# Moving the steps of the pattern weights apart by a group of units, and loading query and key rows twice

## The chip, the cores and the metric

One core of a Trainium2 chip runs one layer of an encoder trunk. The metric is the device time of one execution in microseconds. TensorE (PE) multiplies matrices and transposes, VectorE (DVE) and ScalarE (ACT) work on tiles, GpSimd (POOL) too, and SyncE (SP) issues nearly all transfers (DMAs). Each engine takes its instructions in order; an instruction that has to wait holds up those behind it.

## The reference

For 2048 tokens of width 1024 (float32): RMSNorm and one input projection, whose columns go half to attention and half to a gated recurrence (HGRN2). Both results together go through an output projection, and a mixture of 16 experts follows. The change lies in the attention:

```python
for window, dilation in ((128, 1), (512, 4), (2048, 16)):
    m, den, num = dilated_window_attention(qh, kh, vh, window, dilation, slopes)
    ms.append(m); dens.append(den); nums.append(num)
m_all = jnp.stack(ms)
scale = jnp.exp(m_all - jnp.max(m_all, axis=0, keepdims=True))
numer = jnp.sum(scale[..., None] * jnp.stack(nums), axis=0)
denom = jnp.sum(scale * jnp.stack(dens), axis=0)
return (numer / denom[..., None]).reshape(B, S, ATTN_WIDTH)
```

There are 8 heads of width 64. For each head and token the three patterns give a maximum, a denominator and a numerator. The weight of a pattern is `scale` divided by `denom`.

## The kernel before

Products in float32 are made of three products of high and low halves. The low halves of the activations (`hlo`) lie in DRAM (`lo_d`) and are loaded through a ring of 9 buffers, four for each block of 256 tokens.

The program text does not fix the order on the engines. It is handed to a planner (`schedule_with_timeline_sim=True`, L1307), which issues what is ready in its own reckoning by priority. Priorities come from lanes, in which the text counts them upwards: `first`, `feed` (loads and preparation of projections), `mixer` (recurrence and attention), `fill` (matmuls of projections, which use PE where the mixer leaves it idle).

Attention goes head by head (`att_head`). Within a head, g = 0 to 3 are groups of 512 tokens. `four(pat, n4, ...)` handles four units of 128 queries: scores on PE, table and minimum on DVE (L661), exponential on ACT (L662), transposes on PE (L664), copies (L666, L668), products with the values (L694), and the numerator out of PSUM (L697 to L701). A group has a `four` of pattern 0 and one of pattern 1; all four of pattern 2 come at the end of g = 1. That makes 12 to a head.

The weights of a group of tokens take this way: the statistics of patterns 0 and 2 are stored to DRAM (`st_d`, L758 and L782), because they come out in another arrangement of tokens than is wanted. `weights(g)` loads them (`sg`, L711), works out the weights on DVE and ACT (L717 to L723, tile `cw` with two buffers), stores these (`cw_d`, L724) and loads them spread over the partitions (`wB`, two buffers, L727, two loads). `combine(g)` multiplies and adds on POOL (L732 to L735) and stores the result to `mixt_d` (L737), which the output projection reads later.

`after(k)`, k = 0 to 7, stands after each `four` of patterns 0 and 1. The dictionary `late` says what comes there: `weights(0)` and `weights(1)` at 4, `combine(0)` at 5, `combine(1)` and `weights(2)` at 6; `weights(3)`, `combine(2)` and `combine(3)` at 0, 1 and 2 of the next head.

Query and key rows of the next head come by `att_load` (L538): 128 partitions x 4 rows of 64 floats into the left half of a tile `x4` (four buffers). `att_twice` (L546) copies them on POOL into the right half. `att_turn` transposes the tile on PE (L576), and ACT and DVE write the queries (`qs`, L580, L581) and the high and low halves of the keys (`kh`, `kl`, L585, L586). `queries` copies queries on POOL (`qc`, L620, L623). While heads run, PE fills with projections (L236 to L238) and with the first half of the output projection (`op_mm`, L859 to L861).

Of the kernel before, what the change touches and what calls it, by code (L numbers as in the profile page):

```python
# [23 lines left out]
F32 = mybir.dt.float32  # L24
F32R = mybir.dt.float32r
# [20 lines left out]
def encoder_layer(ctx, tc, x, norm1_w, w_in, q_norm_w, k_norm_w, lb_f, lb_b, o_norm_w, w_out,  # L46
# [80 lines left out]
    def phase0(g):  # L127

        xs = []
        for i in range(2):  # L130
            t = g * 2 + i
            xt = xp.tile([128, D], F32, name="xt", bufs=8)
            sp.dma_start(xt, x[0, t * 128:(t + 1) * 128, :])
            xs.append(xt)
        for xt in xs:
            ss = xp.tile([128, 1], F32, name="ss", bufs=4)
            y = xp.tile([128, 1], F32, name="ssy", bufs=4)
            tm = xp.tile([128, 1], F32, name="sst", bufs=4)
            junk = xp.tile([128, D], F32, name="junk", bufs=2)
            act.activation(junk, xt, AF.Square, accum_out=ss)  # L140
            dve.tensor_scalar(ss, ss, 1.0 / D, EPS, op0=OP.mult, op1=OP.add)
            rsqrt(y, ss, tm)
            dve.tensor_scalar(xt, xt, y, None, op0=OP.mult)
        sl = slice(g * 256, (g + 1) * 256)
        lot = []
        for k in range(0, KC, 2):
            p = (pa, pb)[k // 2 % 2]()
            for j in range(2):
                for i in range(2):
                    c = (2 * j + i) * 128  # L150
                    pe.transpose(p[:, c:c + 128], xs[i][:, (k + j) * 128:(k + j + 1) * 128], ident)
            pv = p.rearrange("p (k t) -> p k t", k=2)
            act.activation(hth[:, k:k + 2, sl], pv, AF.Copy)  # L153
            lo = ring.tile([128, 2, 256], F32R, name="hlo", bufs=9)
            dve.tensor_sub(lo, pv, hth[:, k:k + 2, sl].bitcast(F32))
            sp.dma_start(lo_d.rearrange("k p s -> p k s")[:, k:k + 2, sl], lo.bitcast(F32))
            lot.append(lo)
        return lot
# [44 lines left out]
    def project(cols, kind, ev, begin=False):  # L203

        lots = []
        with (first if begin else feed)():
            if begin:
                lots.append(phase0(0))
            pieces = [prep(cols, kc) for kc in range(KC)]
        for g in range(8):  # L210
            lot = []
            if begin:
                if g < 7:
                    with first():
                        lots.append(phase0(g + 1))
                lot = lots[g]
            with feed():
                for k2 in range(len(lot), 4):
                    t = ring.tile([128, 2, 256], F32R, name="hlo", bufs=9)
                    sp.dma_start(t.bitcast(F32), lo_d.rearrange("k p s -> p k s")[:, k2 * 2:k2 * 2 + 2, g * 256:(g + 1) * 256])  # L220
                    lot.append(t)

            p = pm()
            for b in range(2):
                bs = slice(b * 128, (b + 1) * 128)
                with fill():
                    o = p[:, b * 256:(b + 1) * 256]
                    for kc in range(KC):
                        hi, lo = pieces[kc]
                        hs = hth[:, kc, g * 256:(g + 1) * 256]  # L230
                        ls = lot[kc // 2][:, kc % 2, :]
                        if kind == "t":
                            l, r = (hs[:, bs], ls[:, bs]), (hi, lo)
                        else:
                            l, r = (hi[:, bs], lo[:, bs]), (hs, ls)
                        pe.matmul(o, l[0], r[0], start=kc == 0, stop=False)  # L236
                        pe.matmul(o, l[0], r[1], start=False, stop=False)  # L237
                        pe.matmul(o, l[1], r[0], start=False, stop=kc == KC - 1)  # L238
            with feed():
                ev(g, p)  # L240
# [259 lines left out]
    def att_setup(p):  # L500
# [13 lines left out]
            pool.dma_start(wq[s * 64:(s + 1) * 64, :], q_norm_w.rearrange("o d -> d o"))  # L514
            pool.dma_start(wk[s * 64:(s + 1) * 64, :], k_norm_w.rearrange("o d -> d o"))
        dve.tensor_scalar(wq, wq, -0.125, None, op0=OP.mult)
        T["wq"], T["wk"], T["late"] = wq, wk, {}
        T["qs"] = p.tile([128, S], F32R, name="qs", bufs=1)

        for n in ("kh", "kl"):  # L520
# [11 lines left out]
    def att_load(p, T, h, g):  # L532

        u, s2 = h // 2, h % 2
        for j in range(2):

            x4 = p.tile([128, 4, 128], F32, name="x4", bufs=4)
            sp.dma_start(x4[:, :, :64],  # L538
                         dram_ap(qk_d, (u * S + g * 512) * 256 + 128 * j + 64 * s2,
                                 [[256, 128], [128 * 256, 4], [1, 64]]))  # L540
            T["x4", g, j] = x4

    def att_twice(T, g):
        for j in range(2):
            x4 = T["x4", g, j]
            pool.tensor_copy(x4[:, :, 64:], x4[:, :, :64])  # L546

    def att_values(T, h, g):

# [41 lines left out]
    def att_head(p, T, h):  # L591
# [113 lines left out]
        qcs = {(0, 0): queries(0, 0), (1, 0): queries(1, 0)}  # L705
        late = T["late"]

        def weights(g):
            sg, wB, nt = grp[g]
            for a in (0, 1):  # L710
                sp.dma_start(sg[:, 2 * a].rearrange("p t c -> p (t c)"),  # L711
                             dram_ap(st_d, ((a * 8 + h) * S + 512 * g) * 2, [[8, 128], [1, 8]]))
            w = p.tile([128, 3, 4], F32, name="cw", bufs=2)
            m8 = p.tile([128, 4], F32, name="cm", bufs=2)
            d8 = p.tile([128, 4], F32, name="cd", bufs=2)
            wd = p.tile([128, 3, 4], F32, name="cdd", bufs=2)
            dve.tensor_reduce(m8, sg[:, :, :, 1].rearrange("p a t -> p t a"), axis=AX.X, op=OP.min)  # L717
            dve.tensor_tensor(w, m8[:, None, :].to_broadcast([128, 3, 4]), sg[:, :, :, 1], op=OP.subtract)
            act.activation(w, w, AF.Exp)
            dve.tensor_mul(wd, w, sg[:, :, :, 0])  # L720
            dve.tensor_reduce(d8, wd.rearrange("p a t -> p t a"), axis=AX.X, op=OP.add)
            dve.reciprocal(d8, d8)
            dve.tensor_mul(w, w, d8[:, None, :].to_broadcast([128, 3, 4]))  # L723
            sp.dma_start(dram_ap(cw_d, h * 3 * S + 512 * g, [[4, 128], [S, 3], [1, 4]]), w)  # L724
            wB = p.tile([128, 3, 256], F32, name="wB", bufs=2)
            for hf in range(2):
                sp.dma_start(wB[64 * hf:64 * hf + 64], dram_ap(cw_d, h * 3 * S + 512 * g + 256 * hf, [[0, 64], [S, 3], [1, 256]]))  # L727
            grp[g] = sg, wB, nt

        def combine(g):  # L730
            sg, wB, nt = grp.pop(g)
# [7 lines left out]

        grp = {}  # L740

        def after(k):

            for f in late.pop(k, []):
                f()

        for g in range(4):
            sg = p.tile([128, 3, 4, 2], F32, name="sg", bufs=4)
            nt = p.tile([128, 2, 256], F32, name="nt", bufs=3)
            grp[g] = sg, None, nt  # L750
            st0 = p.tile([128, 4, 2], F32, name="st0", bufs=2)
            if g == 0:
                att_twice(T, 2)
                att_twice(T, 3)
            elif g > 1 and h < 7:
                att_twice(T, g - 2)
            four(0, 4 * g, st0, nt[:, 0])
            sp.dma_start(dram_ap(st_d, (h * S + 512 * g) * 2, [[2, 128], [256, 4], [1, 2]]), st0)  # L758
            after(2 * g)
# [17 lines left out]
            if g == 1:  # L777
# [4 lines left out]
                sp.dma_start(dram_ap(st_d, (8 + h) * S * 2, [[32, 128], [1, 32]]), st2.rearrange("p r c -> p (r c)"))  # L782
                if h < 7:
                    att_v2(T, h + 1)
                late[4] = [lambda: weights(0), lambda: weights(1)]
                late[5] = [lambda: combine(0)]
                late[6] = [lambda: combine(1), lambda: weights(2)]
            if g and h < 7:
                att_values(T, h + 1, g - 1)
                if g == 3:  # L790
                    att_values(T, h + 1, 3)
        late[0] = [lambda: weights(3)]
        late[1] = [lambda: combine(2)]
        late[2] = [lambda: combine(3)]
        if h == 7:
            for k in range(3):
                after(k)


    def op_setup(op):  # L800
        T = {"op": op}
        T["wh"] = op.tile([128, KC, D], F32R, name="woh", bufs=1)
        T["wl"] = op.tile([128, KC, D], F32R, name="wol", bufs=1)

# [17 lines left out]
    def op_weights(T, half):  # L822
        for k in range(4 * half, 4 * half + 4):
# [2 lines left out]
            act.activation(T["wh"][:, k, :], raw, AF.Copy)  # L826
            dve.tensor_sub(T["wl"][:, k, :], raw, T["wh"][:, k, :].bitcast(F32))

    def op_mm(T, c, half, src):

        op = T["op"]
        r = slice(c * 128, (c + 1) * 128)
        with feed():
            mt = op.tile([128, 512], F32, name="mx", bufs=2)
            mtv = mt.rearrange("p (k t) -> p k t", k=4)
            if half:
                sp.dma_start(mt, mix_d[r, :])
            else:
                sp.dma_start(mtv, mixt_d[c // 4].rearrange("(k p) s -> p k s", p=128)[:, :, c % 4 * 128:c % 4 * 128 + 128])
            xt = op.tile([128, D], F32, name="oxt", bufs=3)  # L840
            sp.dma_start(xt, src[r, :])
# [112 lines left out]
    with mixer():  # L954
# [3 lines left out]
        for g in range(4):  # L958
            att_load(ap_, AT, 0, g)
            att_values(AT, 0, g)  # L960
            if g < 2:
                att_twice(AT, g)
                att_turn(AT, g)
    heads(0)
    unit_qk(2)
# [5 lines left out]
    octx = ExitStack()  # L971
    op = octx.enter_context(tc.tile_pool(name="op", bufs=1, side="right"))
    with feed():
        OT = op_setup(op)
        op_weights(OT, 1)
    for c in range(NT):
        op_mm(OT, c, 1, x[0])
# [333 lines left out]
```

## Time and profile before

| | us |
|---|---|
| median of 3 runs | 2851.4 |
| lowest, highest | 2849.88, 2853.11 |
| the profiled execution | 2847.59 |
| its span, first to last instruction | 2845.8 |

| engine | busy us | share of the span |
|---|---|---|
| PE | 2648.8 | 93% |
| DVE | 1779.0 | 63% |
| ACT | 1461.0 | 51% |
| POOL | 329.7 | 12% |

The shares are means over stages with different limits. The projections and the recurrence run to about 860 us, attention with projections beside it from there to about 1480, the output projection and the choice of tokens to about 1700, the experts from there to the end. A wait is read from the instruction that waits and the one that released it.

### The profile page before, as it was taken

What the parts mean: (1) busy time and instruction counts of PE and PEld (TensorE: products, weight loads), DVE (VectorE), ACT (ScalarE), POOL (GpSimd) and SP (SyncE); (2) the same over time, 40 slices, a digit from 0 to 9 for tenths busy, and PEclk for the clock granted to TensorE, in tenths of its full rate; (3) what the DMA queues carried; (4) which work ended last, traced back from release to release, by engine and by line L of the source; (5) the groups of instructions that cost most, each with busy time, mean ns of one, the idle gap of its engine ahead of it and who ended that gap; (6) DMA issues with size and microseconds to landing.
All of it is one profiled execution on the core that took longest, in us unless ns stands there. A gap on an engine that the chain in (4) does not pass through costs nothing.

```text
span 2845.8 us, 61997 instructions
## 1 busy us (share of the span) xinstructions
PE 2648.8 (93%) x24198; PEld 2440.1 (86%) x24198; DVE 1779.0 (63%) x4463; ACT 1461.0 (51%) x3056; POOL 329.7 (12%) x541
## 2 busy tenths in 40 slices
PE   8999999998998888888879959999999999999998
PEld 8899999997998778767766749999999999999997
DVE  6547887878865655665545665555555555555553
ACT  6546667666645545554434534444444444444443
POOL 0000000000012333443320010000000000000000
PEclk9999999999999899999989969999999999999999
DMA  8886777766677566656557616666666666666663
GB/s 301 242 253 209 245 220 240 221 206 211 205 215 160 127 140 146 133 139 150 141 156 254 220 68 211 207 207 207 207 207 207 206 208 207 207 207 207 206 197 103
DMA packets 579861, 554.93 MB, mean 195 GB/s; under 512 B 152416, under 2 KB 533344, under 8 KB 579568
## 3 DMA queue, kind: packets, MB, share of 16 engines
q1 hardware_dynamic: 570032, 517.33, 60.1%
q0 software_dynamic: 9536, 33.64, 5.3%
q8 instruction: 190, 3.11, 0.5%
q14 instruction: 103, 0.84, 0.1%
HBM read 458.11 MB, written 92.73 MB: 194 GB/s over the span
## 4 chain that ended last, share of the span: by engine, by line
PE 72%; DMA 14%; DVE 8%; ACT 2%; SPq 2%; issue 1%; POOL 0%; POOLq 0%; DVEq 0%; ACTq 0%
PE mpg L1227 9%; PE mpg L1229 9%; PE mpg L1228 9%; PE pm L237 5%; PE pm L238 5%; PE pm L236 5%; PE mpy L1262 4%; PE mpy L1264 4%; PE mpy L1263 4%; PE pn L694 2%; DMA gz<-pf_d 2%; PE pb L664 2%; PE pm L860 2%; PE pm L861 2%; PE pm L859 2%
## 5 line engine op out<-in xcount | busy, mean ns | idle before, releaser
L1211 DVE TENSOR_TENSOR mlo<-mraw,mhi 128x1024 fp32r<-128x1024 f32 x384 | 470.1, 1225 | 458.4 <-ACT mhi L1210 457.8
L1210 ACT ACTIVATE mhi<-mraw 128x1024 fp32r<-128x1024 f32 x384 | 406.9, 1060 | 596.9 <-PE mpg L1228 398.6
L1227 PE MATMUL mpg<-xh,mhi 128*128 128x256 f32 x2048 | 579.6, 283 | 0.0
L1229 PE MATMUL mpg<-xh,mlo 128*128 128x256 f32 x2048 | 579.1, 283 | 0.0
L1228 PE MATMUL mpg<-xl,mhi 128*128 128x256 f32 x2048 | 576.5, 282 | 0.0
L1228 PEld LDWEIGHTS mpg<-xl,mhi 128*128 128x128 f32 x2048 | 387.5, 189 | 0.6
L1227 PEld LDWEIGHTS mpg<-xh,mhi 128*128 128x128 f32 x2048 | 386.3, 189 | 1.1 <-ACT xh L1183 0.4
L1229 PEld LDWEIGHTS mpg<-xh,mlo 128*128 128x128 f32 x2048 | 384.0, 187 | 0.0
L236 PE MATMUL pm<-whi,hth 128*128 128x256 f32 x1280 | 364.3, 285 | 16.4 <-ACT ast L178 11.2
L238 PE MATMUL pm<-whi,hlo 128*128 128x256 f32 x1280 | 367.7, 288 | 3.1 <-DMA hlo<-lo_d 3.1
L237 PE MATMUL pm<-wlo,hth 128*128 128x256 f32 x1280 | 367.6, 288 | 1.3 <-DVE wlo L171 1.0
L236 PEld LDWEIGHTS pm<-whi,hth 128*128 128x128 f32 x1280 | 245.4, 192 | 18.5 <-ACT ast L178 11.7
L238 PEld LDWEIGHTS pm<-whi,hlo 128*128 128x128 f32 x1280 | 245.6, 192 | 5.0 <-DMA hlo<-lo_d 4.1
L237 PEld LDWEIGHTS pm<-wlo,hth 128*128 128x128 f32 x1280 | 245.0, 192 | 3.7 <-DVE wlo L171 2.5
L236 PE MATMUL pm<-hth,whi 128*128 128x256 f32 x768 | 219.9, 287 | 2.0 <-ACT hth L153 0.9
L237 PE MATMUL pm<-hlo,whi 128*128 128x256 f32 x768 | 219.4, 286 | 1.6 <-DMA hlo<-lo_d 1.6
L238 PE MATMUL pm<-hth,wlo 128*128 128x256 f32 x768 | 218.0, 285 | 2.4 <-DVE wlo L171 2.3
L1262 PE MATMUL mpy<-mhi,hh 128*128 128x512 f32 x512 | 205.9, 403 | 0.0
L1263 PE MATMUL mpy<-mlo,hh 128*128 128x512 f32 x512 | 203.9, 398 | 0.0
L1264 PE MATMUL mpy<-mhi,hl 128*128 128x512 f32 x512 | 202.9, 396 | 0.0
L238 PEld LDWEIGHTS pm<-hth,wlo 128*128 128x128 f32 x768 | 145.7, 190 | 3.9 <-DVE wlo L171 3.8
L662 ACT ACTIVATE ex<-ex,st 128x256 f32<-128x256 f32 (+1 forms) x256 | 113.6, 446 | 68.4 <-DVE st L661 61.2
(350 smaller groups left out, 5471.4 us busy)
## 6 DMA issues: line engine op xcount, KB each, us to landing
hlo<-lo_d SPq DMA_DIRECT2D x480, 256.0 KB, 4.3
mraw<-in_w_expert_gate_dram SPq DMA_DIRECT2D x64, 1024.0 KB, 5.4
mraw<-in_w_expert_up_dram SPq DMA_DIRECT2D x64, 1024.0 KB, 5.3
mraw<-in_w_expert_down_dram SPq DMA_DIRECT2D x64, 1024.0 KB, 5.0
wraw<-in_w_in_dram SPq DMA_DIRECT2D x128, 128.0 KB, 3.7
out_dram<-oxt SPq DMA_DIRECT2D x32, 512.0 KB, 4.2
pf_d<-est SPq DMA_DIRECT2D x96, 128.0 KB, 4.1
wB<-cw_d SPq DMA_DIRECT2D x64, 192.0 KB, 5.8
```

Of the source, the lines that this page charges most:

```text
L236: pe.matmul(o, l[0], r[0], start=kc == 0, stop=False)
L237: pe.matmul(o, l[0], r[1], start=False, stop=False)
L238: pe.matmul(o, l[1], r[0], start=False, stop=kc == KC - 1)
L662: act.activation(ex[:, c], ex[:, c], AF.Exp, bias=m, scale=-1.0, accum_out=st[:, j, 0:1])
L1210: act.activation(hi, src, AF.Copy)
L1211: dve.tensor_sub(lo, src, hi.bitcast(F32))
L1227: pe.matmul(o, hi[:, k, :], xh[:, k, :], start=k == 0, stop=False)
L1228: pe.matmul(o, hi[:, k, :], xl[:, k, :], start=False, stop=False)
L1229: pe.matmul(o, lo[:, k, :], xh[:, k, :], start=False, stop=k == KC - 1)
L1262: pe.matmul(o, hh[:, f, ts], hi[:, cs], start=f == 0, stop=False)
L1263: pe.matmul(o, hh[:, f, ts], lo[:, cs], start=False, stop=False)
L1264: pe.matmul(o, hl[:, f, ts], hi[:, cs], start=False, stop=f == KC - 1)
```

## The change

The way of the weights is cut into four functions: `fetch` (loads of the statistics), `weights` (arithmetic and store), `spread` (loads of the spread weights) and `combine`. For groups 0 and 1 they stand at positions 4, 5, 6 and 7; for group 2 at 5, 6, 7 and 8; for group 3 at 7, 8, 9 and 10, where 8 to 10 are 0 to 2 of the next head. At one position `combine` goes first. After the last head all that is left is issued at once.

The copy on POOL goes. `att_load` loads the same rows twice, into the left and the right half. The numerators (`nt`) have four buffers in place of three, `hlo` eight in place of nine. The first load of `mix_d` rows for the output projection is issued before its weights.

```diff
-            lo = ring.tile([128, 2, 256], F32R, name="hlo", bufs=9)
+            lo = ring.tile([128, 2, 256], F32R, name="hlo", bufs=8)
...
             x4 = p.tile([128, 4, 128], F32, name="x4", bufs=4)
-            sp.dma_start(x4[:, :, :64],
-                         dram_ap(qk_d, (u * S + g * 512) * 256 + 128 * j + 64 * s2,
-                                 [[256, 128], [128 * 256, 4], [1, 64]]))
+            for c in range(2):
+                sp.dma_start(x4[:, :, 64 * c:64 * c + 64],
+                             dram_ap(qk_d, (u * S + g * 512) * 256 + 128 * j + 64 * s2,
+                                     [[256, 128], [128 * 256, 4], [1, 64]]))
             T["x4", g, j] = x4
-
-    def att_twice(T, g):
-        for j in range(2):
-            x4 = T["x4", g, j]
-            pool.tensor_copy(x4[:, :, 64:], x4[:, :, :64])
...
-        def weights(g):
-            sg, wB, nt = grp[g]
+        def fetch(g):
+            sg = grp[g][0]
             for a in (0, 1):
                 sp.dma_start(sg[:, 2 * a].rearrange("p t c -> p (t c)"),
                              dram_ap(st_d, ((a * 8 + h) * S + 512 * g) * 2, [[8, 128], [1, 8]]))
+
+        def weights(g):
+            sg = grp[g][0]
             w = p.tile([128, 3, 4], F32, name="cw", bufs=2)
...
             sp.dma_start(dram_ap(cw_d, h * 3 * S + 512 * g, [[4, 128], [S, 3], [1, 4]]), w)
+
+        def spread(g):
             wB = p.tile([128, 3, 256], F32, name="wB", bufs=2)
             for hf in range(2):
                 sp.dma_start(wB[64 * hf:64 * hf + 64], dram_ap(cw_d, h * 3 * S + 512 * g + 256 * hf, [[0, 64], [S, 3], [1, 256]]))
-            grp[g] = sg, wB, nt
+            grp[g] = grp[g][0], wB, grp[g][2]
...
+        for g, ks in ((0, (4, 5, 6, 7)), (1, (4, 5, 6, 7)), (2, (5, 6, 7, 8)), (3, (7, 8, 9, 10))):
+            for k, f in zip(ks, (fetch, weights, spread, combine)):
+                late.append((8 * h + k, f is not combine, len(late), f, g))
+
         def after(k):
-
-            for f in late.pop(k, []):
-                f()
+            for t in sorted(t for t in late if t[0] <= 8 * h + k):
+                late.remove(t)
+                t[3](t[4])
...
-            nt = p.tile([128, 2, 256], F32, name="nt", bufs=3)
+            nt = p.tile([128, 2, 256], F32, name="nt", bufs=4)
...
-                late[4] = [lambda: weights(0), lambda: weights(1)]
-                late[5] = [lambda: combine(0)]
-                late[6] = [lambda: combine(1), lambda: weights(2)]
...
-        late[0] = [lambda: weights(3)]
-        late[1] = [lambda: combine(2)]
-        late[2] = [lambda: combine(3)]
         if h == 7:
-            for k in range(3):
-                after(k)
+            after(10)
...
+    def op_rows(T, c):
+        mt = T["op"].tile([128, 512], F32, name="mx", bufs=2)
+        sp.dma_start(mt, mix_d[c * 128:(c + 1) * 128, :])
+        return mt
...
-        OT = op_setup(op)
+        OT = {"op": op}
+        OT["mx"] = op_rows(OT, 0)
+        op_setup(OT)
         op_weights(OT, 1)
```

## Rows read from the trace of the kernel before

**Rows 1.** The page: PE's busy tenths in 40 slices of the span.
```profile
PE   8999999998998888888879959999999999999998
```

**Rows 2.** Stretches: start and end, length, then busy us of each engine, PEclk, DMA.
```profile
core 0: us, PE busy (x) PEld busy (x) DVE busy (x) ACT busy (x) POOL busy (x), PEclk, DMA share, GB/s
860.00:1480.00 620.00, 533.16 (x5017) 468.76 (x5015) 356.99 (x1338) 308.12 (x1076) 222.70 (x430) 0.92 0.60 138
...
1100.00:1130.00 30.00, 30.00 (x318) 27.96 (x318) 20.51 (x83) 21.33 (x81) 12.70 (x21) 1.00 0.66 154
900.00:910.00 10.00, 5.59 (x42) 4.63 (x41) 5.89 (x23) 4.04 (x13) 0.00 (x0) 0.68 0.58 109
...
1150.00:1160.00 10.00, 2.29 (x11) 2.32 (x12) 4.55 (x10) 0.97 (x3) 7.45 (x16) 0.64 0.71 153
```

**Rows 3.** Waits, 850 to 1500: who waited for whom, us, times, longest.
```profile
POOL x L546 <- DMA x<-qk_d: 135.5, 25, 21.9
...
ACT cw L719 <- DVE cw L718: 107.8, 21, 15.8
DVE cm L717 <- DMA sg<-st_d: 105.5, 23, 14.4
...
PE pa L649 <- ACT kh L585: 22.7, 4, 10.5
...
PE pn L694 <- DVE cw L723: 12.2, 3, 6.2
...
DVE cw L718 <- DMA cw_d<-cw: 9.6, 4, 5.3
```

**Rows 4.** Timeline, 997.5 to 1021: start, us, engine, instruction, idle before it.
```profile
995.87 6.38 SPq L727 DMA_DIRECT2D wB<-cw_d  x3
...
998.44 0.19 ACT L662 ACTIVATION_READ_ACCUMULATOR ex<-ex,st 128x1 f32 x1
...
1008.68 0.42 SPq L758 DMA_DIRECT2D st_d<-st  x1
...
1017.75 0.17 DVE L717 TENSOR_REDUCE cm<-sg 128x4 f32<-128x12 f32 x1 [14.45 <-DMA sg<-st_d]
...
1018.27 0.67 ACT L585 ACTIVATE kh<-pb,wk 128x512 fp32r<-128x512 f32 x1
...
1019.00 0.29 PEld L649 LDWEIGHTS pa<-kh,qc 128*128 128x128 f32 x1 [10.71 <-ACT kh L585]
```

**Rows 5.** Timeline of DVE: L717 with its wait, first and last of five.
```profile
903.25 0.17 DVE L717 TENSOR_REDUCE cm<-sg 128x4 f32<-128x12 f32 x1 [6.38 <-DMA sg<-st_d]
...
1154.98 0.17 DVE L717 TENSOR_REDUCE cm<-sg 128x4 f32<-128x12 f32 x1 [8.29 <-DMA sg<-st_d]
```

**Rows 6.** Timeline of SP, 900 to 932: issues in order.
```profile
901.57 1.30 SPq L711 DMA_DIRECT2D sg<-st_d  x3
...
905.01 0.42 SPq L758 DMA_DIRECT2D st_d<-st  x1
```

**Rows 7.** DMA issues: count, KB each, median us to landing; the queue, 850 to 1450.
```profile
hlo<-lo_d SPq DMA_DIRECT2D x480, 256.0 KB, 4.3
...
x<-qk_d SPq DMA_DIRECT2D x64, 128.0 KB, 4.9
...
sg<-st_d SPq DMA_DIRECT2D x64, 4.0 KB, 2.7
...
st_d<-st SPq DMA_DIRECT2D x32, 4.0 KB, 5.7
cw_d<-cw SPq DMA_DIRECT2D x32, 6.0 KB, 4.4
...
q1 hardware_dynamic: 178302, 83.67, 60.4%
```

**Rows 8.** Waits of SP, 850 to 1500.
```profile
SPq L727 <- DMA cw_d<-cw: 25.1, 9, 5.1
```

**Rows 9.** Lines L538 and L546: duration ns min/median/max, first and last start.
```profile
L538 SPq DMA_DIRECT2D x<-qk_d x64: 360/451/1532, 829.6 to 1385.3; - x64
...
L546 POOL COPY x<-x x64: 392/402/902, 835.6 to 1388.5; 128x256 f32<-128x256 f32 x64
```

More of the change, by code (lines that the diff above doesn't have):

```diff
@@ L218, in project @@
                 for k2 in range(len(lot), 4):
-                    t = ring.tile([128, 2, 256], F32R, name="hlo", bufs=9)
+                    t = ring.tile([128, 2, 256], F32R, name="hlo", bufs=8)
                     sp.dma_start(t.bitcast(F32), lo_d.rearrange("k p s -> p k s")[:, k2 * 2:k2 * 2 + 2, g * 256:(g + 1) * 256])
@@ L516, in att_setup @@
         dve.tensor_scalar(wq, wq, -0.125, None, op0=OP.mult)
-        T["wq"], T["wk"], T["late"] = wq, wk, {}
+        T["wq"], T["wk"], T["late"] = wq, wk, []
         T["qs"] = p.tile([128, S], F32R, name="qs", bufs=1)
@@ L740, in att_head @@
         grp = {}
+        for g, ks in ((0, (4, 5, 6, 7)), (1, (4, 5, 6, 7)), (2, (5, 6, 7, 8)), (3, (7, 8, 9, 10))):
+            for k, f in zip(ks, (fetch, weights, spread, combine)):
+                late.append((8 * h + k, f is not combine, len(late), f, g))
         def after(k):
-            for f in late.pop(k, []):
-                f()
+            for t in sorted(t for t in late if t[0] <= 8 * h + k):
+                late.remove(t)
+                t[3](t[4])
         for g in range(4):
             sg = p.tile([128, 3, 4, 2], F32, name="sg", bufs=4)
-            nt = p.tile([128, 2, 256], F32, name="nt", bufs=3)
+            nt = p.tile([128, 2, 256], F32, name="nt", bufs=4)
             grp[g] = sg, None, nt
             st0 = p.tile([128, 4, 2], F32, name="st0", bufs=2)
[L752 to L756, printed above, removed]
             four(0, 4 * g, st0, nt[:, 0])
@@ L791, in att_head, with op_setup @@
                     att_values(T, h + 1, 3)
-        late[0] = [lambda: weights(3)]
-        late[1] = [lambda: combine(2)]
-        late[2] = [lambda: combine(3)]
         if h == 7:
-            for k in range(3):
-                after(k)
-    def op_setup(op):
-        T = {"op": op}
+            after(10)
+    def op_setup(T):
+        op = T["op"]
         T["wh"] = op.tile([128, KC, D], F32R, name="woh", bufs=1)
@@ L833, in op_mm @@
         with feed():
-            mt = op.tile([128, 512], F32, name="mx", bufs=2)
+            mt = T.pop("mx", None) if half else op.tile([128, 512], F32, name="mx", bufs=2)
+            if mt is None:
+                mt = op_rows(T, c)
             mtv = mt.rearrange("p (k t) -> p k t", k=4)
-            if half:
-                sp.dma_start(mt, mix_d[r, :])
-            else:
+            if not half:
                 sp.dma_start(mtv, mixt_d[c // 4].rearrange("(k p) s -> p k s", p=128)[:, :, c % 4 * 128:c % 4 * 128 + 128])
@@ L961, in encoder_layer @@
             if g < 2:
-                att_twice(AT, g)
                 att_turn(AT, g)
```

## The prediction

> **What bounds the kernel now.** The page's slices are read first: from the 25th on, in the experts' stage, TensorE (PE) is full, and the thin places lie before it [rows 1]. Nothing in the change touches that stage, so whatever it is worth must come out of the attention stage, 860 to 1480 us. The table of stretches shows the state there: PE is busy 533.2 of 620 us at a mean granted clock of 0.92, so it idles 86.8 us; a good stretch (1100 to 1130) has it full at clock 1.00, while a few stretches of 10 us stand half or nearly empty, and their clock falls to 0.64 or 0.68 [rows 2]. At the lower of the two levels (1.2 of 2.4 GHz) a matmul takes longer, so a hole costs its own length and some more behind it.
>
> The waits of that stretch come next, to see whose wait ends last. VectorE's (DVE) first instruction of the weights, L717, waits for its statistics to come back from DRAM 23 times, 105.5 us in all; ScalarE's L719 behind it 107.8 us. Among PE's own longest entries are waits for the key evacuation (L585) and for the last weights product (L723), 22.7 and 12.2 us: instructions that are not late by themselves, but stand behind the weights on in-order engines [rows 3]. The timeline of one hole shows it step by step: ScalarE ends the last exponential of a group at 998.63; the issue queue on SP, occupied from 995.87 by three loads of spread weights (6.38 us), then by others, stores the statistics only at 1008.68; DVE's L717 runs at 1017.75 after 14.45 us; the evacuation of the keys L585 is behind L719 on ScalarE; and PE, which needs those keys, starts again after 10.71 us [rows 4]. So the attention stage is bound in turns by PE and by a round trip through DRAM that in-order engines stand in.
>
> **What the order is made of.** The text of the program is not the order on the engines: a planner sorts what is ready by priority, and the text only gives the priority. Three loads of statistics go out at 901.57, before the store at 905.01 behind which all of them are written [rows 6]. Moving a step by one group of four units thus moves its priority; it moves the instruction on its engine only where something else was ready in the planner's reckoning. This is the main uncertainty, and I can't read the new order from the old trace.
>
> **The change part by part.**
>
> *The way of the weights.* A head takes 620 us / 8 = 77.5 us and has 12 groups of four, so one group is worth about 6.5 us. A trip is a store of the statistics (landing 5.7 us after issue) and a load (2.7 us) [rows 7]. With the load one group ahead of the arithmetic, 6.5 us cover 2.7 us, and with the load of groups 2 and 3 one position earlier the store of 5.7 us is covered too. If the engines followed the text, all 23 waits would go. What would they give? In five such stretches (900, 920, 980, 1010 and 1150 us) PE idles 4.41 + 7.92 + 6.24 + 9.00 + 7.71 = 35.3 us [rows 2], and the waits of L717 that make them are 6.38, 8.27, 9.04, 14.45 and 8.29, together 46.4 us [rows 4, 5], so a long wait costs PE 0.76 of its length. The short ones cost less, since PE has projection matmuls to fill with; I take 0.55 over all, 58 us. Ten or so holes each leave PE at the low clock for some microseconds; at 1 us lost in each that is 10 us more. The upper bound of the gain is 68 us, the lower 0. As the planner may keep an instruction where it was, I take half: 34 us.
>
> *The spread weights.* Their two loads a group move one or two groups behind the store, so SP no longer stands in the wait for that store: 25.1 us in 9 waits [rows 8]. Behind these stand the loads of query and key rows, and the store and load of the next statistics, as in [rows 4]. This is part of the 34 us, not added to it. The combining on GpSimd (POOL) comes later, off the path: PE reads none of it before the output projection. The fourth buffer for the numerators only makes room for this. Group 2's spread loads stand right behind the combining of groups 0 and 1, whose two buffers they need, so SP can wait there for POOL; before, they stood behind the combining of group 1 in the same way. I add nothing for these.
>
> *Query and key rows loaded twice.* Removed: 64 copies on POOL, 402 ns each, 25.7 us, and POOL's waits of 135.5 us in them [rows 3, 9]. POOL is not the bound, being busy 222.7 of 620 us [rows 2]; a row's way to PE loses the 0.40 us of its copy and gains the 0.451 us of a second issue, so zero, between a gain and a loss of 0.4 us a load, which a load fetched a group ahead hides. Added: 64 loads. Each takes SP 0.451 us, 28.9 us in the stage, or 3.6 us per head [rows 9]. Each is 512 rows of 256 bytes, 32,768 packets more; the hardware queue's 178,302 packets in 600 us took 60.4% of 16 engines, 32.5 ns each [rows 7], so the new ones take 32,768 x 32.5 ns / 16 = 67 us of all engines, and the share goes from 0.60 to about 0.72. Cost on the path: none where the rows are fetched a group ahead; at the other end the whole SP time, 28.9 us, if SP's lateness is what every hole waits for. The hole in [rows 4], where a store was some 10 us late, says that SP's time matters in part of the holes; I take a sixth, 5 us.
>
> The Trainium skill, "DMA: Bandwidth & Descriptors", Specifications and Why small descriptors are slow, wants at least 512 bytes in a descriptor and charges a 256-byte one 11 cycles where 8 carry data. At the 850 MHz of that page this is an estimate of 12.9 ns a packet and 27 us of all engines, against 67 us by the row; either way it speaks against loading twice, and by the page the 5 us would be 3.
>
> *Weights closer together.* The arithmetic of groups 0 and 1 moves from position 4 to 5, that of group 2 stays at 6. The tile for the weights has two buffers, so group 2 needs group 0's store landed (4.4 us after issue) [rows 7], with one group between instead of two. Before, this wait already occurs 4 times, 9.6 us, the longest 5.3 [rows 3]. From 0 to 8 heads x 5.3 = 42 us; one group, 6.5 us, is longer than the landing, so I take 5 us.
>
> *Small edits.* One buffer fewer of the low halves of the activations: eight hold two whole blocks of a projection, so while PE works through one, the next has its 4.3 us to land [rows 7]. I take nothing; a loss of a few microseconds would show in PE's waits for them. The first load of mixed rows ahead of the output weights: a load takes about 5 us to land here (4.9 for the rows) [rows 7], at the one place where the projection starts, which PE's fill covers or not; 0 to 5 us gained, taken as 0. The tail after the last head keeps its chain of store, load, store, load, and costs and gains nothing.
>
> Sum: -34 + 5 + 5 = -24 us. The profiled execution took 2847.6 us (span 2845.8, 1.8 around it), 3.8 under the median of 2851.4. From its own time: 2823.6; as a median, **2827 us**.
>
> **The rivals.**
>
> *The planner keeps the order.* The instructions become ready at the same reckoned time and find an idle engine as before. For it: DVE is busy only 357 of 620 us [rows 2], so there is seldom another candidate. Against it: SP's order does change, as the row loads are new. Time: 2846 to 2857.
>
> *SP and the queues become the bound (slower).* Place: SP, between the store of pattern 2 and the next head's first group, where 8 issues of rows become 16 per head. Price: the late store in [rows 4] gets later by 3.6 us per head of issue and by longer landings; 28.9 us at most, less what still goes from the DVE waits, 12 us: about +17, 2868. It decides if SP, already late by 10 us in a hole, has no slack in most heads. If the weight tile's wait comes up in every head as well, 42 us, the time passes 2880.
>
> *All waits go.* The full 68 us, less the 10 of cost: 2793. For it: the covers worked out above are all longer than the trips.
>
> **How the numbers follow.** A measurement of this kernel tells 0.2%, some 5.7 us, from no change. Forecast, a partial gain of 7 to 45 us: 0.42, own range 2806 to 2844. All waits gone: 0.14. No change: 0.14. Slower: 0.30, mostly 2858 to 2880. So faster 0.56, same 0.14, slower 0.30. The range leaves out the best of the full gain and the worst of the slower case: 2788 to 2868.
>
> **What would show it.** Right: L717's waits for its load fall from 105.5 us to under 50; the empty 10 us stretches become fewer and PE's granted clock in the stage rises over 0.94; POOL shows no copies of rows. The doubled load right: 128 issues, landing near 5 to 6 us, DMA share about 0.7. Wrong: L717 waits as long as before; or L718 waits for the weights' store in most heads; or the evacuations wait directly for the row loads, so that PE's holes stay and only change their name; or the stage is the same and another stage moved, which none of these steps explains.

## The result and the profile after

The changed kernel takes 2877.1 us, the median of 4 runs (2875.2 to 2881.4), where the kernel before takes 2851.2 in the same comparison: a ratio of 1.0092, 95% interval 1.0075 to 1.0110. It is slower by 25.9 us. I had predicted 2827, and the range ended at 2868. The profiled execution is the slowest of the four, 2881.4 us with a span of 2879.6, so its trace holds 33.8 us more than that of before.

Waits of the changed kernel, 850 to 1500 us, as in [rows 3] (line 716 is the old L717, 717 the old L718, 690 the old L694, 722 the old L723):

```profile
DVE cm L716 <- DMA sg<-st_d: 132.9, 23, 15.9
ACT cw L718 <- DVE cw L717: 130.3, 23, 14.9
...
PE pn L690 <- DVE cw L722: 13.4, 2, 8.8
...
PE pm L858 <- DVE cw L717: 12.3, 1, 12.3
...
DVE cw L717 <- DMA cw_d<-cw: 11.2, 5, 4.0
...
PE pn L690 <- DVE cw L717: 7.5, 1, 7.5
PE pn L690 <- DVE cd L720: 7.3, 1, 7.3
...
PE pn L690 <- DVE cdd L719: 6.8, 1, 6.8
```

The wait that the change was to shorten is as frequent as before, 23 times, and longer: 132.9 us for 105.5. By the profile, 13.4 + 12.3 + 7.5 + 7.3 + 6.8 = 47.3 us of PE's waits, 6 of them, now end with instructions of the weights, where before there were 12.2 us in 3. PE reads none of their results; what it needs stands behind them on DVE, as the copies of L664 do from 1073.74 on in the hole below. POOL's waits in the copies of rows are gone with the copies.

The stretch of [rows 2], 860 to 1480:

```profile
860.00:1480.00 620.00, 522.06 (x4948) 463.13 (x4946) 347.39 (x1328) 309.45 (x1069) 185.73 (x352) 0.92 0.66 147
```

PE is busy 11.1 us less than before, at the same clock of 0.92. The DMA share is 0.66 where it was 0.60; I had said 0.72.

Query and key rows of the changed kernel, then its hardware queue (850 to 1450), beside [rows 9] and [rows 7]:

```profile
L539 SPq DMA_DIRECT2D x<-qk_d x128: 359/502/3797, 832.0 to 1417.8; - x128
```

```profile
q1 hardware_dynamic: 207609, 89.95, 66.9%
...
x<-qk_d SPq DMA_DIRECT2D x123, 128.0 KB, 5.0
```

The 128 loads land as fast as the 64 did (5.0 us). What has grown is the time that SP spends on issuing one: median 0.502 us for 0.451, the longest 3.8.

Where the time went is read from the stores of statistics, which mark the heads. Kernel before, then the changed one (first and last start):

```profile
L758 SPq DMA_DIRECT2D st_d<-st x32: 360/419/1599, 877.3 to 1448.3; - x32
```

```profile
L759 SPq DMA_DIRECT2D st_d<-st x32: 359/378/2627, 885.3 to 1478.9; - x32
```

Of the 33.8 us, 8.0 are there when the first group of the first head is stored, 22.6 come in the heads (571.0 us before, 593.6 after), and 3.2 behind them. The split is of these two traces and not a rule, since the output projection's matmuls fill the heads to a different degree: with the value loads on POOL (below) 448 of them lie in the heads, for 312 before, and the heads take 622.6 us and what follows them 1359.1, for 1397.5 before.

A hole of the changed kernel, timeline 1056 to 1075 (start, us, engine, instruction, idle before it):

```profile
1056.55 3.19 SPq L554 DMA_DIRECT2D vp<-v_d  x5
1059.83 1.11 SPq L738 DMA_DIRECT2D mixt_d<-nt  x2
1060.99 1.52 SPq L554 DMA_DIRECT2D vp<-v_d  x3
1062.55 1.94 SPq L707 DMA_DIRECT2D sg<-st_d  x2
1064.60 1.80 SPq L554 DMA_DIRECT2D vp<-v_d  x4
1066.49 0.58 SPq L550 DMA_DIRECT2D vp<-v_d  x1
1067.17 0.56 SPq L783 DMA_DIRECT2D st_d<-st  x1
1069.31 0.34 SPq L707 DMA_DIRECT2D sg<-st_d  x1
...
1070.17 0.46 SPq L707 DMA_DIRECT2D sg<-st_d  x1
```

```profile
1057.43 0.19 ACT L658 ACTIVATION_READ_ACCUMULATOR ex<-ex,st 128x1 f32 x1
```

```profile
1060.41 0.08 DVE L657 DVE_READ_ACCUMULATOR2_ANT st<- 128x1 f32 x1
1070.97 0.17 DVE L716 TENSOR_REDUCE cm<-sg 128x4 f32<-128x12 f32 x1 [10.48 <-DMA sg<-st_d]
```

```profile
1074.57 1.12 PE L690 MATMUL pn<-eT,vp 128*64 128x64 f32 x16 [8.84 <-DVE cw L722]
```

The last statistic of pattern 2 is there at 1057.6 (ACT). SP stores it only at 1067.17: of the nine and a half microseconds between, other issues take 7.6, and SP's pauses among them the rest. Its load follows at 1069.3 and 1070.2, DVE's weights run after 10.48 us, and PE starts again after 8.84. It is a hole of the same kind as in [rows 4], with value loads in the place of the spread weights' loads (there the weights of group 3 stood in it, here those of groups 0 and 1). And it shows where the weights stand: L716 comes right behind the minima of pattern 0 of this group (`st<-`, 1060.41) and ahead of those of pattern 1, though the text now puts it behind both. In DVE's instruction stream the weights of groups 0 and 1 stand ahead of pattern 1 of group 2 in 7 of 8 heads in the changed kernel, as they did in 7 of 8 before.

### The profile page after: what moved, and what is told of

It is laid out like the page before. It is cut to its first block, busy times and chain, and to the rows that moved or that the text cites. A ratio compares the mean times of both kernels' runs of the same rounds, so it can differ in the third digit from the quotient of the medians.

```text
span 2879.6 us, 61971 instructions
## 1 busy us (share of the span) xinstructions
PE 2656.7 (92%) x24198; PEld 2447.7 (85%) x24198; DVE 1772.3 (62%) x4463; ACT 1465.3 (51%) x3056; POOL 304.3 (11%) x477
## 4 chain that ended last, share of the span: by engine, by line
PE 74%; DMA 14%; DVE 6%; SPq 2%; ACT 2%; issue 2%; POOL 1%; POOLq 0%; DVEq 0%; ACTq 0%
PE mpg L1227 9%; PE mpg L1229 9%; PE mpg L1228 9%; PE pm L238 6%; PE pm L237 6%; PE pm L236 6%; PE mpy L1262 4%; PE mpy L1264 4%; PE mpy L1263 4%; PE pn L690 2%; DMA st_d<-st 2%; PE pb L660 2%; PE pm L859 2%; PE pm L858 2%; DMA gz<-pf_d 2%
## 5 line engine op out<-in xcount | busy, mean ns | idle before, releaser
L236 PE MATMUL pm<-whi,hth 128*128 128x256 f32 x1280 | 364.5, 286 | 16.3 <-ACT ast L178 10.4
L238 PE MATMUL pm<-whi,hlo 128*128 128x256 f32 x1280 | 369.0, 289 | 6.2 <-DMA hlo<-lo_d 6.2
L237 PE MATMUL pm<-wlo,hth 128*128 128x256 f32 x1280 | 365.7, 287 | 0.0
L238 PEld LDWEIGHTS pm<-whi,hlo 128*128 128x128 f32 x1280 | 245.7, 192 | 8.9 <-DMA hlo<-lo_d 7.9
L237 PEld LDWEIGHTS pm<-wlo,hth 128*128 128x128 f32 x1280 | 244.8, 191 | 1.4 <-DVE wlo L171 0.4
L237 PE MATMUL pm<-hlo,whi 128*128 128x256 f32 x768 | 221.0, 288 | 2.6 <-DMA hlo<-lo_d 2.4
L238 PE MATMUL pm<-hth,wlo 128*128 128x256 f32 x768 | 219.2, 286 | 3.8 <-DVE wlo L171 3.8
L690 PE MATMUL pn<-eT,vp 128*64 128x64 f32 (+1 forms) x2048 | 114.6, 246 | 53.8 <-DVE cw L722 13.4
L690 PEld LDWEIGHTS pn<-eT,vp 128*64 128x64 f32 x2048 | 87.4, 141 | 78.3 <-ACT qs L576 14.1
```

Of the source, the lines that this page charges most:

```text
L690: pe.matmul(pnum[64 * hf:64 * hf + 64, cols], vp[:, units[u][3][i], :], e, start=i == 0, stop=i == len(units[0][3]) - 1)
```

## The experiments

Three theories. A: the 64 added loads make SP, or the queues, the bound, and the moved steps bring nothing because they stay where they were. B: the moved steps themselves cost, by another order on SP. C: any edit deals the planner's order anew, and the time moves by some 10 us either way. The runs were made on four chips, where the kernel before takes 2859 to 2861 us; each is compared as a ratio to the kernel before on its own chip, with 95% intervals.

**The parts by themselves.** The ring of `hlo` with 8 buffers alone:

```diff
-name="hlo", bufs=9
+name="hlo", bufs=8
```

> The kernel before with eight buffers instead of nine for the low halves of the activations, nothing else. Theory A (SP and the queues have become the bound, by the 64 added loads): 2851 to 2856, since this touches neither. Theory B (the moved steps cost, by another order on SP): the same. Theory C (any edit makes the planner deal the order anew, and the time moves by some 10 us with no relation to the edit): anywhere between 2840 and 2866, and the attention stage changes as much as the projections. By its own price: PE's waits for these tiles (6.2 us at L238 in the changed kernel against 3.1) say +3 to +6.

Measured: 1.0032 (1.0019 to 1.0044), 2867.8 us. Rows loaded twice alone, without the copies on POOL:

```diff
-            sp.dma_start(x4[:, :, :64], dram_ap(qk_d, ...))
+            for c in range(2):
+                sp.dma_start(x4[:, :, 64 * c:64 * c + 64], dram_ap(qk_d, ...))
...
-            pool.tensor_copy(x4[:, :, 64:], x4[:, :, :64])
```

> The kernel before with query and key rows loaded twice and no copy on POOL; steps of the weights, buffers and the rest as before. Theory A: 15 to 25 us slower, 2866 to 2876. Theory B: no change, 2846 to 2856. Theory C: between 2840 and 2866.

Measured: 1.0069 (1.0050 to 1.0088), 2880.5 us. The four steps alone (with the fourth `nt`, and the ring of 8 that makes room for it):

```diff
+        for g, ks in ((0, (4, 5, 6, 7)), (1, (4, 5, 6, 7)), (2, (5, 6, 7, 8)), (3, (7, 8, 9, 10))):
+            for k, f in zip(ks, (fetch, weights, spread, combine)):
+                late.append((8 * h + k, f is not combine, len(late), f, g))
```

> The changed kernel with rows loaded once and copied on POOL, and without the early load of mixed rows: so the moved steps of the weights, four buffers of numerators and eight of low halves. Theory A: 2852 to 2860, the ring's cost alone, as the instructions of the weights stand at the same places on VectorE. Theory B: 15 to 25 us slower than before, 2866 to 2876. Theory C: between 2840 and 2876.

Measured: 1.0027 (1.0013 to 1.0041), 2867.1 us, the same as the ring alone. The early load of mixed rows alone:

```diff
+        OT["mx"] = op_rows(OT, 0)
         op_setup(OT)
```

> The kernel before with the first load of mixed rows ahead of the output weights, nothing else. Theories A and B: 2846 to 2853. Theory C: up to 10 us either way, which for one load moved would be the planner's doing alone.

Measured: 0.9996 (0.9984 to 1.0008), 2858.8 us.

So the parts are +0.69% for the rows, +0.32 for the ring, -0.05 for the steps and -0.04 for the mixed rows; their sum, 0.92%, is the whole change. B falls, since the steps cost or bring nothing beyond some 0.2%, the room that the two intervals leave. C falls as the main cause: two edits that change the order without adding work (the steps beside the ring alone, and the mixed rows) move the time by 0.05%, with the same room. For the ring C is not ruled out: in the trace of the ring of 8, PE idles 93.8 us in the heads (from the first to the last store of pattern 0's statistics) where it idled 77.6 before, and its waits for the keys, part of which stand behind the weights on ACT, have doubled from the 22.7 us in 4 of [rows 3]:

```profile
PE pa L649 <- ACT kh L585: 45.5, 5, 12.8
```

**What the doubled loads cost by.** The second load of each pair from POOL's queue:

```diff
-            for c in range(2):
-                sp.dma_start(x4[:, :, 64 * c:64 * c + 64], ...)
+            for c, q in ((0, sp), (1, pool)):
+                q.dma_start(x4[:, :, 64 * c:64 * c + 64], ...)
```

> The kernel before with the rows loaded twice, the second load of each pair issued by POOL on its own queue instead of by SP. The packets are as many as in the run with both loads on SP, which took 0.69% more than the kernel before; SP's issues are those of the kernel before. If the cost is SP's issuing and its queue's order, the time comes back to within 0.2% of the kernel before; if it is the 256-byte packets on the 16 engines, it stays at +0.5 to +0.8%; if it is only that every edit deals the order anew, any value between -0.3% and +0.5% is as likely.

Measured: 1.0007 (0.9994 to 1.0021), 2862.6 us. 64 further issues that carry one row each and that nothing reads:

```diff
+            xd = p.tile([128, 64], F32, name="xd", bufs=1)
+            sp.dma_start(xd[:1], dram_ap(qk_d, ..., [[256, 1], [1, 64]]))
```

> The kernel before with 64 more DMA issues on SP, each beside a row load and of one row of 256 bytes that nothing reads; the copies by POOL stay. No packets to speak of are added (64 to 580,000). If SP's issue time is the cost (64 times 0.45 us, 29 us of SP), the time rises by 0.4 to 0.7%; if the packets are the cost, it stays within 0.2% of the kernel before.

Measured: 1.0026 (1.0013 to 1.0038), 2867.1 us. Both loads from SP, with POOL's copies kept:

> The kernel before with the rows loaded twice from SP and POOL's copies kept as well (they write over the second load). Issues, packets and readers' waits of the doubled loads are all there, and only the copies' removal is not. If the added loads are the cost, +0.5 to +0.9% over the kernel before, as with the loads alone (+0.69%); if the cost came from taking the copies off POOL (its later products then wait directly, in another order), within 0.2%.

Measured: 1.0108 (1.0086 to 1.0130), 2887.8 us: the loads are the cost, and the copies' removal is not. It may even be a gain, for with the copies the loads cost 0.39% more than without (the intervals just meet). The second load from ACT's queue (`(1, act)` in the edit with POOL's):

> The kernel before with the rows loaded twice, the second load of each pair issued by ACT on its own hardware queue. The packets are those of the run with both loads on SP (256 bytes each, which POOL's queue had packed into fewer). If the cost is SP's issuing, the time is within 0.25% of the kernel before, less what 64 issues cost ACT; if it is the 256-byte packets of the hardware queues, it stays at +0.5 to +0.8%.

Measured: 1.0117 (1.0097 to 1.0138), 2890.2 us. This didn't tell packets and issues apart, for ACT pays another price. Waits of PE in that kernel, 850 to 1500:

```profile
PE pb L663 <- ACT ex L661: 37.8, 12, 8.5
```

It was 1.3 us before: ACT's exponentials now share their engine with 64 issues of 0.37 us each, and with these issues' waits. But the two queues give one answer, in their rows of 850 to 1450 (packets, MB, share of 16 engines), ACT's and then POOL's:

```profile
q10 hardware_dynamic: 31152, 7.74, 6.2%
```

```profile
q0 software_dynamic: 2795, 7.63, 6.0%
```

The second loads take the same time of the DMA engines from either queue, 6.0 to 6.2%, and from POOL's the kernel is not slower. In POOL's run the two queues together take 62.1 + 6.0 = 68.1%, more than the one queue with both loads on SP (65.0%), and yet its time is 0.62% shorter. So these 0.62% are not the engines' time. Nor do the added packets in SP's queue delay the trip: with both loads on SP the store and the load of statistics land in 5.0 and 2.7 us (medians, 850 to 1450), where it was 5.7 and 2.7 before. What the engines' time may cost beside these 0.62%, hidden behind a gain from the copies' removal, no run separates. The Trainium skill, "Trainium Kernel Development and Optimization", Key Constraints, says that issuing from several engines saves nothing but issue time, since all queues run on the same DMA engines; by that rule the 0.62% between the two runs is SP's issue time, and the two shares agree with it. Last, the doubled loads as they are, with the value loads of the dilated pattern taken off SP:

```diff
-                sp.dma_start(v0[32 * r + lo:32 * r + hi, b:b + n, :64],
+                pool.dma_start(v0[32 * r + lo:32 * r + hi, b:b + n, :64],
```

> The kernel before with the rows loaded twice from SP (1.0069), with the 160 or so small loads of the values of the dilated pattern (line 557, most of the 139 us that SP spends on issuing value loads between 850 and 1450 us) issued by POOL. The doubled loads stay as they are, packets and all. If the cost of the doubled loads is SP's time, which this gives back and more, the time comes back to the kernel before or below it (0.992 to 1.001); if it is the rows' packets in SP's queue and on the engines, it stays at 1.005 to 1.008. A stall of POOL behind a load that waits for its buffer would raise it further.

Measured: 1.0004 (0.9992 to 1.0017), 2859.3 us. They are 192 loads, not 160. The hardware queue, 850 to 1450, is fuller than with the doubled loads alone (65.0%), though with fewer packets (208,718 there):

```profile
q1 hardware_dynamic: 189783, 91.69, 68.1%
```

With 82 us less of SP's time than with both loads alone, the cost is gone. It is no more than gone, though SP now issues 34 us less than in the kernel before. Either these loads count for less than the rows, or POOL takes a part back (an issue takes 0.55 us there, and POOL waits for PE in them for 43.3 us); this run doesn't tell. (What the kernel before would gain by this edit alone wasn't tried.)

Summed over SP's single issues from 850 to 1450, issuing takes SP 377.8 us in the kernel before, 425.8 with the rows twice and 343.5 in the last run. (A row of the timeline merges issues that follow each other and counts the pauses between them, so that a sum over its rows comes out larger.) The row loads are 31.0 us of it before and 79.5 with both, the single rows of the second test 18.3. So 48.5 us more of SP cost 0.69% (19.7 us) and 18.3 us cost 0.26% (7.4 us): 0.4 us for each microsecond of added issues, in both. (The intervals leave a good deal of room, 14 to 25 us and 4 to 11; and in the run with the single rows SP's other issues take less, so that its sum is 378.7, as before. The place of the added issues may count there and not the sum; this wasn't tested.)

**Steps that are really behind.** The changed kernel, with an order edge from each late step to the last unit of the four before it (an added dependency: the planner may not put the step ahead of that unit):

```diff
+                last["dve"] = dve.tensor_tensor_reduce(e, s_, tab, ...)
+                last["act"] = act.activation(ex[:, c], ex[:, c], AF.Exp, ...)
...
+                with tc.issue_after(ins(last["dve"])), tc.issue_after(ins(last["act"])):
                     t[3](t[4])
```

> The changed kernel, with each late step (fetch, weights, spread, combine) held by an order edge behind the last unit of the four before it on DVE and ACT: in DVE's order the weights of groups 0 and 1 then stand behind the second half of group 2 in all heads and not ahead of it, as the planner had put them in 7 of 8. In the changed kernel DVE waits for the statistics' way back (line 716) 132.9 us in 23 waits between 850 and 1530 us. If the moved steps failed to pay because the planner kept their place, those waits fall below 50 us here, and the time falls below that of the changed kernel by up to the 34 us that I had put in for them (2843 to 2870 where the changed kernel has 2877). Rival: DVE and PE were not waiting for this on the path that sets the end, so that the waits go and the time stays within 6 us of the changed kernel.

Measured: 1.0032 (1.0017 to 1.0046), 2867.7 us, where the changed kernel has 1.0092. DVE in that kernel, at the place of the hole above (here `sg<-` marks the minima of pattern 1):

```profile
1064.04 0.08 DVE L660 DVE_READ_ACCUMULATOR2_ANT sg<- 128x1 f32 x1
1066.29 0.17 DVE L719 TENSOR_REDUCE cm<-sg 128x4 f32<-128x12 f32 x1 [2.16 <-DMA sg<-st_d]
1066.72 0.17 DVE L719 TENSOR_REDUCE cm<-sg 128x4 f32<-128x12 f32 x1 [0.27 <-DMA sg<-st_d]
```

The weights stand behind pattern 1 now, and the wait of 10.48 us is 2.16. PE's waits for instructions of the weights, 47.3 us, are none. DVE's waits for the statistics fall from 132.9 to 31.2 us, those for the weights' store rise from 11.2 to 53.0. The same edges with the steps alone, rows loaded once:

> The kernel before with the steps of the weights' way alone (nt 4, hlo 8, rows loaded once and copied by POOL), and each late step held by an order edge behind the last unit of the four before it on DVE and ACT. Without the edges this kernel took 0.27% more than the kernel before and the ring of 8 alone 0.32% more. With the edges the changed kernel fell to +0.32%. If the steps pay once they really stand later in DVE's order, this one comes to -0.1 to -0.6% (2842 to 2857 us beside 2859); if the edges paid in the changed kernel only by easing SP, which the doubled loads had filled, it stays at +0.1 to +0.4%.

Measured: 0.9943 (0.9924 to 0.9961), 2844.0 us: faster than both kernels. The edges alone turn 1.0027 into 0.9943, 24 us. DVE's waits for the weights' transfers in it, 850 to 1500:

```profile
DVE cw L724 <- DMA cw_d<-cw: 41.0, 8, 9.9
DVE cm L723 <- DMA sg<-st_d: 34.6, 10, 9.3
```

Without the edges they were 12.1 and 99.2. So the waits fell by 35.7 us together, and the wait for the weights' store took over part of the place. Four buffers for `cw` take that one away:

```diff
-            w = p.tile([128, 3, 4], F32, name="cw", bufs=2)
+            w = p.tile([128, 3, 4], F32, name="cw", bufs=4)
```

> The kernel with the steps of the weights' way alone and order edges (0.9943 of the kernel before), with 4 buffers for cw instead of 2. With the edges, the weights of three groups stand within one four, and DVE waits for the store of the weights two groups earlier (line 724 of that kernel, 41.0 us in 8 waits between 850 and 1530 us): the wait that I had named as the price of weights closer together. If it lies on the path, the time falls by another 0.3 to 1.2% of the kernel before (0.983 to 0.991); if DVE has slack there, it stays at 0.994, within 0.2%.

Measured: 0.9959 (0.9945 to 0.9974), 2846.9 us. No gain. The wait for the store is gone, but that for the statistics is longer, so that only 15.7 of the 75.6 us went:

```profile
DVE cm L723 <- DMA sg<-st_d: 59.9, 16, 11.6
```

**Versions.** Edges and the second load from POOL:

> The changed kernel with the same order edges and the second load of each pair on POOL's queue. If the two effects add (edges -0.6% against the changed kernel, the load off SP -0.62%), it comes to -0.3% against the kernel before, 2846 to 2854 us beside 2859; if both relieve the same thing, SP, and so don't add, it stays within 0.2% of the kernel before.

Measured: 0.9973 (0.9960 to 0.9987), 2850.3 us. That is what the sum of the two effects gives, but still 0.3% more than with the rows loaded once and copied. The same with 9 buffers of `hlo` and 3 of `x4`:

> The kernel with order edges and the second load on POOL's queue, with 9 buffers for hlo again and 3 for the query and key rows (4 before), so that the memory is enough. If the ring of 8 costs its 0.32% here too and the third row buffer is not missed, 0.2 to 0.4% below the same kernel with the ring of 8; if the row loads now wait for their buffer, at or above it.

Measured: 0.9939 (0.9923 to 0.9955), 2842.5 us: the two sizes together are worth 0.34% here, about what the ring cost alone. Rows once, edges, four `cw`, the ring of 9 and 3 buffers of `x4`:

> The same with the ring of hlo at 9 again and 3 buffers for the query and key rows. With the second load on POOL's queue this pair of sizes gave 0.34%. If the ring's cost adds to the rest, 0.2 to 0.4% below the kernel with 4 buffers for cw alone.

Measured: 0.9941 (0.9925 to 0.9958), 2839.7 us. Against the kernel with four `cw` alone that is 0.18%, with intervals that overlap. Three versions stand at 0.994; the one with the fewest edits is the steps with order edges.

## Why the prediction was wrong

*The reading of the hole held, its weight didn't.* The attention stage is bound in turns by PE and by the way through DRAM, and the late party in the hole is SP, in [rows 4] as in the hole above. I read that SP was some 10 us late, and then charged SP's time at a sixth.

*The way of the weights: -34 us, measured about -1.* The step that failed is "as the planner may keep an instruction where it was, I take half". The planner kept the arithmetic of groups 0 and 1, the only one that moves in the text, in its place in 7 of 8 heads, and the half became nothing. By groups (0 with 1, then 2, then 3), DVE idles ahead of the first instruction of the weights for 30.5, 23.0 and 54.2 us before, for 60.2, 8.3 and 64.8 in the changed kernel, and for 10.4, 11.0 and 20.8 with the steps and edges alone. So group 2, whose load the text moved ahead of its arithmetic, did gain, and the others lost more than that. Half of the idle time before belongs to group 3, whose arithmetic the change leaves at its place in the text; the planner put it ahead of the next head's first `four` in all 7 heads before and still in 4 of 7 after. The sizes behind the 34 us were fair: with the edges, DVE's waits fell by 35.7 us and the time by 24, 0.67 us for each if all of the gain came from them (I had 0.55 over all and 0.76 for long ones). Against the ring alone, the steps with edges give 0.9943 / 1.0032 = 0.9911, some 25 us. The full 68 us were out of reach in these runs: about 75 us of DVE's waits stay in new places, and taking away the 41 of them that hang on the weights' store gave nothing, as most of it came back as waits for the statistics.

*Spread weights.* SP's waits for the weights' store were 25.1 us in 9, and are 16.2 in 10 in the changed kernel.

*Query and key rows loaded twice: +5 us, measured about +20.* Two factors of one term were too small. The added SP time was 28.9 us by the median of one issue; it is 48.5, since an issue takes 0.65 us in the mean with both loads (79.5 / 123) and 0.51 before, where the median of 0.451 leaves out the long ones. And the share that reaches the end is 0.4, not a sixth. The copies, put at nothing, may have been worth something: kept beside the doubled loads they cost 0.39%, so that the loads without that gain may cost up to 31 us. The packets, of which I had worked out 67 us of all engines, are not what 18 of these 20 us went on: a second load takes the engines 6.0 to 6.2% from POOL's queue and ACT's, and from POOL's it costs 0.07% with the copies gone. By ACT's row a packet takes 0.062 x 16 x 600 us / 31,152 = 19.1 ns, less than my 32.5. The estimate of 12.9 ns from the Trainium skill, "DMA: Bandwidth & Descriptors", Why small descriptors are slow, was nearer to this than my row, and still well under it. (The 3 us that the prediction draws from it don't follow: its 5 us came from SP's issue time, which a price of packets doesn't touch.)

*Weights closer together: +5 us, measured about 0.* In the changed kernel the wait is 11.2 us for 9.6, as the arithmetic didn't move. With edges it comes up as I had bounded it (41.0 us; bound 42). Four buffers take it away and the time is no better; but as the statistics' wait grew by 25.3 us in its place, this doesn't show what the wait alone costs.

*Small edits: 0, measured +9.* The ring of 8 costs 0.32%. PE's waits for `hlo` at L237 and L238 rise from 1.6 + 3.1 to 2.9 + 5.7 us with the ring alone, 3.9 of the 9. The rest stays open; the trace of the ring alone shows 16.2 us more of PE's idle time in the heads, with longer waits for the keys, so a newly dealt order may be a part of it. The mixed rows were rightly put at nothing.

Measured sum: -1 + 20 + 9 - 1 = +27, against 25.9. Of the rivals, two came true together: the planner kept DVE's order, and SP became the bound. I had given the first the price of no change and taken 12 us of gain off the second, so that 2868 was its usual end; with no gain from the steps the same sum, 28.9 from SP, would have ended at 2880.

The signs held: L717 (now L716) waits no shorter than before, and PE's granted clock stays at 0.92, as I had named for the wrong case.

What stays open: why the copies on POOL beside doubled loads cost 0.39% more than the doubled loads alone, what the engines' time costs beside SP's, and how the ring of 8 comes to 9 us.

## What to carry to other kernels

Where a planner orders the engines, a step that is moved in the text has not been moved until the engine's instruction stream shows it in another place; look there first, and tie it with an order edge where it must stand behind. Before adding issues to a queue that serves a round trip, add up how much of the stage its engine already spends issuing (here 378 of 600 us): the price of one more lies in what stands behind it, here some 0.4 us for each microsecond of added rows. Measure a buffer that is given up for another edit by itself; here it cost 9 us, the half of what the rows cost.

## What was not expected of the hardware

POOL's queue writes the same 512 rows of 256 bytes in far fewer packets, as the trace counts them: 2795 for 58 loads (48 each, 2.7 KB), where ACT's takes 31,152 for 59, and both occupy the DMA engines equally long (6.0 and 6.2%). The issue itself takes 0.760 us on POOL, 0.367 on ACT and 0.42 to 0.51 on SP (medians of the runs); the cheapest one gave the slowest kernel, where PE's waits for ACT's exponentials rose from 1.3 to 37.8 us.
